# Dilated attention of a two-block model: normalising the outputs instead of the probabilities, in interleaved steps

## The chip, the cores and the metric

The kernel runs on one core of a Trainium2 chip, in one launch. The metric is the device time of that core in microseconds (us), from which the program is judged by the median of several runs. TensorE is called PE here, its weight loads PEld, VectorE DVE, ScalarE ACT, GpSimd POOL and SyncE SP; SP issues most of the transfers (DMAs).

## The reference

The model is two blocks, one after the other, on 1024 tokens of width 1024. The change touches the attention of the second block only: 8 heads of width 64, each a mixture of three causal windows of dilation 1, 4 and 16. The kernel takes the mixture as one softmax per head: the three branches share their scores, and a pair of positions that lies in several branches counts as often, which the kernel puts into a table `bias` of one row set per head (distance times slope, less the logarithm of the count).

```python
for window, dilation in ((128, 1), (512, 4), (2048, 16)):
    s = q·k / 8 + bias                # causal, keys t, t-d, ..., t-window
    m = max(s); p = exp(s - m); denom = sum(p)
    o = (p @ v) / denom;  lse = m + log(denom)
w = softmax(lse over the branches)
attn = sum(w * o over the branches)
```

All products are wanted to nearly full float32 accuracy. The kernel gets it by splitting an operand into a rounded part (type float32r, which PE takes at its fast rate) and the remainder, and adding the products.

## The kernel before

The program works through mixer 1, an MLP, a gate, a feed-forward layer, mixer 2 (where the attention is) and another feed-forward layer. In mixer 2 the projections `qk` and `v`, a state-space part and its gate (`glu`) come ahead of the attention, the output projection (`down`, its first rows at L455) behind it. The method `attention` (L1629) is called once, by `mixer2`.

The order on each engine is found by a scheduler while the program is built: it takes the instructions in the order in which the code issues them as priorities, gives out the buffers of the pools, and writes one fixed queue per engine. At run time each engine takes its queue in order and waits at each instruction for what it needs. So the order of the Python calls, and which pool a tile is in, set the queues.

The tiles come from pools with a fixed number of buffers: `u` (`self.u`, 32 buffers of 128x1024), `t` (`self.tmp`, 5 of 128x512), small ones (`self.sm`), and 8 PSUM banks (`self.bank`). A tile waits until an older one in its pool has been read for the last time.

One pair of heads is one tile `q` and one tile `k` of 128x1024: head `a` = 0 in partitions 0 to 63, `a` = 1 in 64 to 127.

- `heads_in` (L1552) makes, for both heads of a pair at once, the operands of the scores: `qq` holds the rounded queries in the head's own half of the partitions and the remainder in the other half; `kd` holds the rounded keys in both halves, `kl` the remainder of the keys in both. ACT makes the rounded ones (L1560, L1561), POOL the remainders (L1563, L1564), and a DMA brings each key tile's other half (L1562, L1565).
- `head_v` (L1569) makes `vv`, the rounded values of a head and their remainder side by side (ACT L1573, DVE L1574).
- `softmax` (L1577) does half of a head, four blocks of 128 queries, of which block `qb` sees (qb + 1) x 128 keys. Per block: two score matmuls per piece of keys (L1596, L1597), a DVE instruction that adds the bias, writes `P` and keeps the minimum (L1599, the scores are negated), the exponential on ACT with its row sum `den` (L1602), the reciprocal of the sum on DVE (L1603), and the multiplication of the whole row by it on POOL (L1604).
- `values` (L1607) does the output of a half head: for each block of 128 keys (`kt`) it transposes up to four blocks of `P` on PE (L1619), splits the result into `ph` on ACT (L1621) and `pl` on DVE (L1622), and adds two matmuls with `vv` to the bank `po` (L1623, L1624). At the end the two halves of `po` are added into `at` (ACT L1626, DVE L1627).
- `attention` prepares the pair after the current one at each pair's first head, calls `softmax` per half head and holds three `values` jobs back.

The prediction also names L1516, the last multiplication of `glu` (tile `yt`), and L1499 and L1496, which split a tile into `hi` and `lo`.

Of the kernel before, what the change touches and what calls it, by code (L numbers as in the profile page):

```python
# [22 lines left out]
H = 512  # L23
# [89 lines left out]
class Z:  # L113
# [3 lines left out]
    late = "s"  # L117
# [60 lines left out]
class ZS(Z):  # L178
# [4 lines left out]
    late = "u"  # L183
# [64 lines left out]
class Model:  # L248
# [1300 lines left out]
                else:  # L1549
                    self.nc.scalar.activation(o, i, AF.Copy)  # L1550

    def heads_in(self, q, k):  # L1552


        nc = self.nc
        res = []
        for a in range(2):
            me, other = slice(64 * a, 64 * a + 64), slice(64 - 64 * a, 128 - 64 * a)
            qq, kd, kl = self.u("qq", F32R), self.u("kd", F32R), self.u("kl", F32R)
# [17 lines left out]
    def softmax(self, ops, bias, half):  # L1577

        nc = self.nc
        qq, kd, kl = ops  # L1580
        if half:
            ps = [self.u("P") for _ in range(4)]
        else:
            two = [self.u("P", shape=[P, 2, H]) for _ in range(2)]
            ps = [two[c // 2][:, c % 2] for c in range(4)]
        mx, den = self.sm("mx", 8), self.sm("den", 4)
        for c, p in enumerate(ps):
            qb = 4 * half + c
            w = (qb + 1) * P
            o = 896 - qb * P  # L1590
            cuts = [0, w] if w <= H else ([0, 384, w] if w < 896 else [0, H, w])
            init = 3.0e38
            for n, (k0, k1) in enumerate(zip(cuts, cuts[1:])):
                pp = self.bank()[:, : k1 - k0]
                qs = slice(qb * P, (qb + 1) * P)
                nc.tensor.matmul(pp, qq[:, qs], kd[:, k0:k1], start=True, stop=False)  # L1596
                nc.tensor.matmul(pp, qq[:, qs], kl[:, k0:k1], start=False, stop=True)  # L1597
                m = mx[:, c : c + 1] if n == len(cuts) - 2 else mx[:, 4 + c : 5 + c]
                nc.vector.tensor_tensor_reduce(out=p[:, k0:k1], in0=pp, in1=bias[:, o + k0 : o + k1], scale=1.0,  # L1599
                                               scalar=init, op0=ALU.add, op1=ALU.min, accum_out=m)  # L1600
                init = m
            nc.scalar.activation(p[:, :w], p[:, :w], AF.Exp, scale=-1.0, bias=mx[:, c : c + 1], accum_out=den[:, c : c + 1])  # L1602
            nc.vector.reciprocal(den[:, c : c + 1], den[:, c : c + 1])  # L1603
            nc.gpsimd.tensor_scalar(out=p[:, :w], in0=p[:, :w], scalar1=den[:, c : c + 1], scalar2=None, op0=ALU.mult)  # L1604
        return ps

    def values(self, vv, a, ps, half, at):  # L1607


        nc = self.nc  # L1610
        po = self.bank("po")
        me, other = slice(64 * a, 64 * a + 64), slice(64 - 64 * a, 128 - 64 * a)
# [12 lines left out]
        t = self.tmp("vo")  # L1625
        nc.scalar.activation(t[me], po[other], AF.Copy)  # L1626
        nc.vector.tensor_tensor(at[me, half * H : half * H + H], po[me], t[me], op=ALU.add)  # L1627

    def attention(self, qk):  # L1629

        at, late = [], []
        ops = [self.heads_in(*qk[0])]
        for j in range(4):
            at.append(self.u("at"))
            for a in range(2):
                h = 2 * j + a
                bias = self.raw(self.a["bias"][h], name="bias", tag="xr")
                if a == 0 and j < 3:
                    ops.append(self.heads_in(*qk[j + 1]))
                vv = self.head_v(h)  # L1640
# [89 lines left out]
```

## Time and profile before

| | |
|---|---|
| median of 3 runs | 3058.43 us (3047.64 to 3059.11) |
| profiled execution | 3056.01 us, its span 3054.2 us |
| busy in the span | PE 93%, PEld 75%, DVE 59%, ACT 43%, POOL 26% |
| mean granted PE clock | 0.968 of full speed |

The profile shows one execution: each instruction with its engine, start and end, its line in the code and the tiles that it writes and reads (`po<-ph,vv`), the idle time of an engine ahead of an instruction and what ended it. PE is the engine with the most work: 40 slices of the span show it at 0.8 or more nearly all the time, and at 0.7 in two slices side by side near 0.7 of the span, where POOL is at its busiest.

### The profile page before, as it was taken

How to read it: one execution, taken by the hardware profiler on the slowest of the kernel's cores; microseconds unless marked ns; L12 is line 12 of the kernel's file. 1: busy time of each engine (PE TensorE's matmuls, PEld its weight loads, DVE VectorE, ACT ScalarE, POOL GpSimd, SP SyncE). 2: the span in 40 equal slices, each digit the busy share in tenths (PEclk: the TensorE clock that was granted, in tenths of full speed). 3: DMA queues.
4: the chain of work that ended last, by engine and by line, in shares of the span. 5: the costliest groups of instructions: out<-in, count | busy, mean ns of one | idle time of the engine just before them, and what ended most of it. 6: DMA issues, size and time to landing. Idle time of an engine off the chain costs nothing. (4 is left out here: it accounts for less than half of the span.)

```text
span 3054.2 us, 33886 instructions
## 1 busy us (share of the span) xinstructions
PE 2828.5 (93%) x12585; PEld 2303.4 (75%) x12585; DVE 1797.1 (59%) x2561; ACT 1320.1 (43%) x1921; POOL 784.1 (26%) x626
## 2 busy tenths in 40 slices
PE   8998999989979989999989999997789999998997
PEld 7777877767757867778777878886677778777776
DVE  4586655575767366666667561417735756565445
ACT  5446554442335473323324362236655533332343
POOL 3320222200211221111122041349854112111001
PEclk9999999999989999999999999999899899999999
DMA  4114344474466123454466562423113244446645
GB/s 145 57 47 138 131 145 152 156 259 160 166 233 220 56 90 106 153 164 151 164 222 237 207 222 81 155 83 111 42 49 131 87 152 159 159 153 207 225 160 200
DMA packets 198200, 452.93 MB, mean 148 GB/s; under 512 B 20533, under 2 KB 25233, under 8 KB 198033
## 3 DMA queue, kind: packets, MB, share of 16 engines
q1 hardware_dynamic: 193424, 433.97, 41.9%
q10 hardware_dynamic: 4608, 16.78, 1.4%
q8 instruction: 99, 1.62, 0.2%
q14 instruction: 69, 0.56, 0.1%
HBM read 316.51 MB, written 129.99 MB: 146 GB/s over the span
## 5 line engine op out<-in xcount | busy, mean ns | idle before, releaser
L701 PE MATMUL b<-tt,wh 128*128 128x512 f32 x2128 | 686.2, 403 | 74.0 <-ACT tt L687 64.4
L541 PE MATMUL b<-zh,wh 128*128 128x512 f32 x1680 | 646.9, 398 | 35.4 <-ACT wh L481 25.6
L541 PE MATMUL b<-zh,wl 128*128 128x512 f32 x1680 | 625.3, 393 | 4.5 <-ACT wl L511 4.0
L541 PE MATMUL b<-zl,wh 128*128 128x512 f32 x1560 | 615.2, 395 | 8.4 <-DVE zl L211 8.4
L701 PEld LDWEIGHTS b<-tt,wh 128*128 128x128 f32 x2128 | 409.3, 194 | 181.5 <-ACT tt L687 73.8
L701 PE MATMUL b<-tt,wl 128*128 128x512 f32 x1064 | 424.1, 399 | 0.0
L541 PEld LDWEIGHTS b<-zh,wh 128*128 128x128 f32 x1680 | 319.8, 191 | 123.9 <-ACT wh L481 38.8
L541 PEld LDWEIGHTS b<-zh,wl 128*128 128x128 f32 x1680 | 318.2, 190 | 75.5 <-ACT wl L511 6.7
L541 PEld LDWEIGHTS b<-zl,wh 128*128 128x128 f32 x1560 | 296.4, 190 | 73.9 <-DVE zl L211 13.4
L688 DVE TENSOR_TENSOR wl<-sd,wh 128x1024 fp32r<-128x1024 f32 x140 | 167.6, 1197 | 190.3 <-ACT wh L687 190.3
L482 POOL TENSOR_TENSOR wl<-raw,wh 128x1024 fp32r<-128x1024 f32 x51 | 123.3, 2418 | 526.1 <-ACT wh L481 486.6
L701 PEld LDWEIGHTS b<-tt,wl 128*128 128x128 f32 x1064 | 206.7, 194 | 43.6
L481 ACT ACTIVATE wh<-raw 128x1024 fp32r<-128x1024 f32 x120 | 127.2, 1060 | 238.4 <-DMA raw<-in_f_in 95.2
L352 POOL TENSOR_TENSOR wl<-raw,wh 128x1024 fp32r<-128x1024 f32 (+1 forms) x58 | 142.7, 2465 | 322.0 <-ACT wh L351 290.2
L687 ACT ACTIVATE wh<-sd 128x1024 fp32r<-128x1024 f32 x140 | 141.5, 1011 | 154.6 <-DMA sd<-hs 111.9
L383 POOL TENSOR_SCALAR v<-ss 128x1 f32<-128x1 f32 x80 | 47.9, 599 | 472.5 <-ACT junk L376 466.3
L619 POOL TENSOR_TENSOR hw<-h 128x512 f32<-128x512 f32 x38 | 60.2, 1583 | 421.1 <-DVE h L1165 188.1
L687 ACT ACTIVATE tt<-wd 128x1024 fp32r<-128x1024 f32 x92 | 94.6, 1028 | 150.3 <-DVE wd L669 133.1
L505 DVE TENSOR_TENSOR s<-raw 128x512 f32<-128x512 f32 x60 | 82.2, 1370 | 107.5 <-DMA raw<-in_f_in 100.6
L482 DVE TENSOR_TENSOR wl<-raw,wh 128x1024 fp32r<-128x1024 f32 x69 | 88.7, 1286 | 84.2 <-ACT wh L481 43.2
L351 ACT ACTIVATE wh<-raw 128x1024 fp32r<-128x1024 f32 (+1 forms) x58 | 59.5, 1031 | 168.2 <-issue 42.7
L688 DVE TENSOR_TENSOR tt<-wd,tt 128x1024 fp32r<-128x1024 f32 x92 | 110.2, 1198 | 27.6 <-ACT tt L687 26.8
(358 smaller groups left out, 5003.4 us busy)
## 6 DMA issues: line engine op xcount, KB each, us to landing
sd<-hs SPq DMA_DIRECT2D x126, 512.0 KB, 5.5
raw<-in_f_in SPq DMA_DIRECT2D x94, 512.0 KB, 3.7
wd<-in_w_down SPq DMA_DIRECT2D x64, 512.0 KB, 6.3
raw<-in_f_out SPq DMA_DIRECT2D x44, 512.0 KB, 3.6
tw<-raw SPq DMA_DIRECT2D x44, 512.0 KB, 2.9
td<-tw SPq DMA_DIRECT2D x40, 512.0 KB, 6.3
hs<-h SPq DMA_DIRECT2D x38, 512.0 KB, 3.1
hs<-hw SPq DMA_DIRECT2D x38, 512.0 KB, 3.0
```

The source lines that it names most:

```text
L351: nc.scalar.activation(h, r, AF.Copy)
L352: nc.gpsimd.tensor_tensor(l, r, h.bitcast(F32), op=ALU.subtract)
L383: nc.gpsimd.tensor_scalar(out=v, in0=ss, scalar1=1.0 / D, scalar2=EPS, op0=ALU.mult, op1=ALU.add)
L481: nc.scalar.activation(hi.rearrange("p a b -> p (a b)"), x, AF.Copy)
L482: eng.tensor_tensor(lo.rearrange("p a b -> p (a b)"), x, hi.bitcast(F32).rearrange("p a b -> p (a b)"), op=ALU.subtract)
L505: v.tensor_tensor(s1, a21, a22, op=ALU.add)
L541: self.mark = nc.tensor.matmul(bank, w, x, start=start and k == 0 and i == 0, stop=k == 3 and i == 2, skip_group_check=True)
L619: g.tensor_tensor(wt[:, 1], x[:, 1], y[:, 0], op=ALU.subtract)
L687: nc.scalar.activation(hi[:, :n], x[:, :n], AF.Copy)
L688: v.tensor_tensor(lo[:, :n], x[:, :n], hi.bitcast(F32)[:, :n], op=ALU.subtract)
L701: self.mark = nc.tensor.matmul(bank, x[:, c, ts], y[:, c], start=start and k == 0, stop=stop and k == 2, skip_group_check=True)
```

## The change

`heads_in` for a pair becomes `head_in` for one head. It first issues two DMAs that copy the keys of the head to both halves of a float32 tile `k2`; the rest is returned as two functions, one for `qq`, one for `kd` and `kl`, which now cover all 128 partitions and need no DMA behind them. The method `attention` calls these, and `head_v`, one at a time between the steps of the head ahead.

`softmax` and `values` become generators. `attention` advances them by turns: a step of `values` is one block of keys, a step of `softmax` one block of queries. A `values` job now starts two half heads behind its `softmax` (LAG = 2), at most two are pending instead of three.

The probabilities are no longer multiplied. Per half head one POOL instruction takes the reciprocals of `den` (a power with exponent -1, 128x4), a DMA writes them as a row of 512 to DRAM (4 bytes at a time, since it transposes), a second brings that row to all partitions (tile `inv`), and at the end of `values` DVE multiplies the output by it. `ph` and `pl` become the two halves of one tile in the pool of 32.

```diff
+    def head_in(self, q, k, a, res):
+        nc = self.nc
+        me, other = slice(64 * a, 64 * a + 64), slice(64 - 64 * a, 128 - 64 * a)
+        two = self.u("k2")
+        for to in (me, other):
+            nc.sync.dma_start(out=two[to], in_=k[me])
+        def left():
+            qq = self.u("qq", F32R)
             nc.scalar.activation(qq[me], q[me], AF.Copy)
-            nc.scalar.activation(kd[me], k[me], AF.Copy)
-            nc.sync.dma_start(out=kd.bitcast(F32)[other], in_=kd.bitcast(F32)[me])
             nc.gpsimd.tensor_tensor(qq[other], q[me], qq.bitcast(F32)[me], op=ALU.subtract)
-            nc.gpsimd.tensor_tensor(kl[me], k[me], kd.bitcast(F32)[me], op=ALU.subtract)
-            nc.sync.dma_start(out=kl.bitcast(F32)[other], in_=kl.bitcast(F32)[me])
-            res.append((qq, kd, kl))
-        return res
+            res.append(qq)
+        def right():
+            kd, kl = self.u("kd", F32R), self.u("kl", F32R)
+            nc.scalar.activation(kd, two, AF.Copy)
+            nc.gpsimd.tensor_tensor(kl, two, kd.bitcast(F32), op=ALU.subtract)
+            res.extend((kd, kl))
+        return [left, right]
...
@@ softmax
             nc.scalar.activation(p[:, :w], p[:, :w], AF.Exp, scale=-1.0, bias=mx[:, c : c + 1], accum_out=den[:, c : c + 1])
-            nc.vector.reciprocal(den[:, c : c + 1], den[:, c : c + 1])
-            nc.gpsimd.tensor_scalar(out=p[:, :w], in0=p[:, :w], scalar1=den[:, c : c + 1], scalar2=None, op0=ALU.mult)
-        return ps
+            yield
+        nc.gpsimd.tensor_tensor(den, den, self.mone, op=ALU.pow)
+        row = self.pd.tile([4, P], F32, name="den", tag="den", bufs=4)
+        inv = self.tmp("inv")
+        nc.sync.dma_start(out=row.rearrange("c q -> q c"), in_=den)
+        nc.sync.dma_start(out=inv, in_=row.rearrange("c q -> (c q)").partition_broadcast(P))
+        ps.append(inv)
...
@@ values
-            ph, pl = self.tmp("ph", dt=F32R), self.tmp("pl", dt=F32R)
+            both = self.u("ph", F32R, [P, 2, H])
+            ph, pl = both[:, 0], both[:, 1]
...
+            if kt < last:
+                yield
         t = self.tmp("vo")
         nc.scalar.activation(t[me], po[other], AF.Copy)
-        nc.vector.tensor_tensor(at[me, half * H : half * H + H], po[me], t[me], op=ALU.add)
+        nc.vector.tensor_tensor(t[me], po[me], t[me], op=ALU.add)
+        nc.vector.tensor_tensor(at[me, half * H : half * H + H], t[me], ps[4][me], op=ALU.mult)
...
@@ attention
-                for half in range(2):
-                    ps = self.softmax(ops[j][a], bias, half)
-                    late.append((vv, a, ps, half, at[j]))
-                    if len(late) > 3:
-                        self.values(*late.pop(0))
-        while late:
-            self.values(*late.pop(0))
+        for n in range(16 + self.LAG):
...
+            for k in range(nk):
+                if val:
+                    next(val, None)
+                if soft and k * 4 % nk == 0:
+                    next(soft)
+                    if k * 4 // nk in (1, 3) and todo and (half or k * 4 // nk == 1 or len(todo) > 2):
+                        todo.pop(0)()
+            if soft:
+                next(soft, None)
```

What this does to the queues is shown at three places. On POOL, in the first heads, the queue before is a run of multiplications of `P`, with the preparation of a pair (`qq`, `kl`) between two runs:

```order
L1604 TENSOR_SCALAR P<-P,den 128x640
L1604 TENSOR_SCALAR P<-P,den 128x768
L1604 TENSOR_SCALAR P<-P,den 128x896
L1604 TENSOR_SCALAR P<-P,den 128x1024
L1563 TENSOR_TENSOR qq<-qk,qq 64x1024
L1564 TENSOR_TENSOR kl<-qk,kd 64x1024
L1563 TENSOR_TENSOR qq<-qk,qq 64x1024
```

and now it is one preparation step and one power of 128x4 by turns:

```order
L1571 TENSOR_TENSOR kl<-k_15429,kd 128x1024
L1614 TENSOR_TENSOR den<-den,mone 128x4
L1565 TENSOR_TENSOR qq<-qk,qq 64x1024
L1614 TENSOR_TENSOR den<-den,mone 128x4
L1571 TENSOR_TENSOR kl<-k_15639,kd 128x1024
```

All 64 multiplications are gone from it. On PE, at the second half of a head's outputs, the queue before has one block of transposes between the first two output matmuls (`idn` is the identity of a transpose, `kd` and `kl` are score matmuls):

```order
L1623 MATMUL po<-ph,vv 128x512
L1619 MATMUL b<-idn,P 128x128 x21
L1624 MATMUL po<-pl,vv 128x512
L1619 MATMUL b<-idn,P 128x128
L1623 MATMUL po<-ph,vv 128x512
L1624 MATMUL po<-pl,vv 128x512
```

and now (L1639 reads `pl`, which is part of the tile `ph`):

```order
L1638 MATMUL po<-ph,vv 128x512
L1606 MATMUL b<-kd,qq 128x384
L1607 MATMUL b<-kl,qq 128x384
L1606 MATMUL b<-kd,qq 128x256
L1607 MATMUL b<-kl,qq 128x256
L1633 MATMUL b<-idn,P 128x128 x8
L1606 MATMUL b<-kd,qq 128x384
L1607 MATMUL b<-kl,qq 128x384
L1606 MATMUL b<-kd,qq 128x384
L1607 MATMUL b<-kl,qq 128x384
L1639 MATMUL po<-ph,vv 128x512
L1633 MATMUL b<-idn,P 128x128 x8
```

Score matmuls have moved between the transposes. On SP, in the middle of the attention, the queue before holds bias tables and key copies only:

```order
L1562 DMA kd<-kd 64x1024 x2
L307 DMA bias<-in_bias 128x1024
L1565 DMA kl<-kl 64x1024 x2
L307 DMA bias<-in_bias 128x1024
```

and now, per head, two transfers of the reciprocals to DRAM (`den`, 128x4 in single elements), each with the broadcast that needs it (`inv`):

```order
L1617 DMA den<-den 128x4x1
L1618 DMA inv<-den 128x512
L1560 DMA k_15639<-qk 64x1024 x2
L307 DMA bias<-in_bias 128x1024
L1617 DMA den<-den 128x4x1
L1618 DMA inv<-den 128x512
```

The key copies and bias tables of later heads stand behind an `inv`, which waits for its `den` to land.

## Rows read from the trace of the kernel before

**Rows 1.** The page's 40 equal slices of the span: busy tenths of PE.
```profile
PE   8998999989979989999989999997789999998997
```

**Rows 2.** Timeline, last two jobs of `values`: start, us, instruction, idle before it.
```profile
2239.98 0.33 PE L1624 MATMUL po<-pl,vv 128*128 128x128 f32 x1
...
2253.02 0.69 DVE L1627 TENSOR_TENSOR at<-po,vo 64x512 f32<-64x512 f32 x1 [1.04 <-ACT vo L1626]
```

**Rows 3.** Stretches: us, then busy PE, PEld, DVE, ACT, POOL; clock, DMA share, GB/s.
```profile
2118.00:2140.00 22.00, 18.79 (x113) 16.25 (x112) 19.57 (x64) 15.99 (x38) 21.59 (x12) 1.00 0.19 49
2157.00:2180.00 23.00, 19.45 (x114) 16.52 (x112) 19.65 (x61) 16.62 (x38) 22.59 (x13) 1.00 0.19 46
2140.00:2157.00 17.00, 10.24 (x55) 8.84 (x53) 10.57 (x31) 13.73 (x28) 17.00 (x10) 0.80 0.23 62
2203.00:2230.00 27.00, 21.29 (x127) 17.96 (x127) 23.21 (x75) 20.48 (x48) 19.15 (x11) 1.00 0.12 40
2079.84:2252.40 172.56, 127.47 (x674) 107.08 (x672) 124.06 (x377) 122.18 (x263) 144.79 (x79) 0.89 0.19 58
```

**Rows 4.** Groups by line, POOL, 2080 to 2253: count, busy us, mean ns, idle before.
```profile
L1604 POOL TENSOR_SCALAR P<-P,den 128x640 f32<-128x640 f32 (+5 forms) x64 | 109.5, 1734 | 11.9 <-DVE den L1603 11.0 <-PE b L1597 0.7
L1563 POOL TENSOR_TENSOR qq<-qk,qq 64x1024 fp32r<-64x1024 f32 x4 | 9.9, 2471 | 0.3
```

**Rows 5.** Waits, 2080 to 2253, PE and ACT: us in total, times, longest.
```profile
PE po L1623 <- ACT ph L1621: 34.0, 17, 5.0
PE b L1619 <- POOL P L1604: 5.8, 3, 3.7
ACT ph L1621 <- PE po L1624: 18.7, 31, 2.1
```

**Rows 6.** Timeline, POOL and PE, 2095 to 2120.
```profile
2095.37 24.53 POOL L1604 TENSOR_SCALAR P<-P,den 128x512 f32<-128x512 f32 x13
...
2109.05 0.33 PE L1619 MATMUL b<-idn,P 128*128 128x128 f32 x1 [3.71 <-POOL P L1604]
```

**Rows 7.** Timeline, ACT and PE, 2146 to 2152.
```profile
2146.74 1.04 ACT L1560 ACTIVATE qq<-qk 64x1024 fp32r<-64x1024 f32 x1
...
2149.71 1.04 ACT L1561 ACTIVATE kd<-qk 64x1024 fp32r<-64x1024 f32 x1
...
2151.43 0.79 PE L1623 MATMUL po<-ph,vv 128*128 128x512 f32 x1 [4.98 <-ACT ph L1621]
```

**Rows 8.** Two lines of the code (POOL, DVE): count, duration ns min/median/max, first and last start.
```profile
L384 POOL TENSOR_TENSOR r<-v,mh x80: 547/548/1627, 6.5 to 3045.9; 128x1 f32<-128x1 f32 x80
...
L1574 DVE TENSOR_TENSOR vv<-v,vv x8: 677/1045/2328, 2062.7 to 2209.0; 128x512 fp32r<-128x512 f32 x8
```

**Rows 9.** Timeline, DVE, 2088 to 2094.
```profile
2088.20 0.15 DVE L1603 RECIPROCAL den<-den 128x1 f32<-128x1 f32 x1
2088.28 0.53 DVE L1599 CUSTOM_DVE_ANT_0 P<-b,bias 128x384 f32<-128x384 f32 x1
...
2093.20 0.74 DVE L1599 CUSTOM_DVE_ANT_0 P<-b,bias,mx 128x512 f32<-128x512 f32 x1
```

**Rows 10.** Groups by line, DVE, 2080 to 2253.
```profile
L1627 DVE TENSOR_TENSOR at<-po,vo 64x512 f32<-64x512 f32 x15 | 10.3, 686 | 9.1 <-ACT vo L1626 9.0
L1516 DVE TENSOR_TENSOR yt<-gs,yt 128x512 f32<-128x512 f32 x3 | 6.0, 1986 | 1.2 <-ACT gs L1515 1.2
```

**Rows 11.** DMA issues of the whole program: KB each, median us to landing.
```profile
raw<-in_pT SPq DMA_DIRECT2D x2, 512.0 KB, 10.2
s5l<-kz SPq DMA_DIRECT2D x64, 32.0 KB, 2.2
dsk<-in_s5d SPq DMA_DIRECT2D x1, 2.0 KB, 9.1
g<-in_rows SPq DMA_DIRECT2D x3, 512.0 KB, 3.9
```

**Rows 12.** Timeline, SP, one issue.
```profile
2093.98 0.33 SPq L307 DMA_DIRECT2D bias<-in_bias  x1
```

More of the change, by code (lines that the diff above doesn't have):

```diff
@@ L1550, in v_proj @@
                     self.nc.scalar.activation(o, i, AF.Copy)
-    def heads_in(self, q, k):
+    def head_in(self, q, k, a, res):
         nc = self.nc
[L1556 to L1559, printed above, removed]
+        me, other = slice(64 * a, 64 * a + 64), slice(64 - 64 * a, 128 - 64 * a)
[4 more added lines that the diff above has]
+            qq = self.u("qq", F32R)
             nc.scalar.activation(qq[me], q[me], AF.Copy)
-            nc.scalar.activation(kd[me], k[me], AF.Copy)
-            nc.sync.dma_start(out=kd.bitcast(F32)[other], in_=kd.bitcast(F32)[me])
             nc.gpsimd.tensor_tensor(qq[other], q[me], qq.bitcast(F32)[me], op=ALU.subtract)
-            nc.gpsimd.tensor_tensor(kl[me], k[me], kd.bitcast(F32)[me], op=ALU.subtract)
-            nc.sync.dma_start(out=kl.bitcast(F32)[other], in_=kl.bitcast(F32)[me])
-            res.append((qq, kd, kl))
-        return res
+            res.append(qq)
[5 more added lines that the diff above has]
+        return [left, right]
     def head_v(self, h):
@@ L1575, in head_v, with softmax @@
         return vv
-    def softmax(self, ops, bias, half):
+    def softmax(self, ops, bias, half, ps):
         nc = self.nc
@@ L1581, in softmax @@
         if half:
-            ps = [self.u("P") for _ in range(4)]
+            ps.extend(self.u("P") for _ in range(4))
         else:
             two = [self.u("P", shape=[P, 2, H]) for _ in range(2)]
-            ps = [two[c // 2][:, c % 2] for c in range(4)]
+            ps.extend(two[c // 2][:, c % 2] for c in range(4))
+        four = list(ps)
         mx, den = self.sm("mx", 8), self.sm("den", 4)
-        for c, p in enumerate(ps):
+        for c, p in enumerate(four):
             qb = 4 * half + c
@@ L1624, in values @@
             nc.tensor.matmul(po[:, sl], vv[:, kt, :], pl[:, sl], start=False, stop=kt == last)
+            if kt < last:
+                yield
         t = self.tmp("vo")
         nc.scalar.activation(t[me], po[other], AF.Copy)
-        nc.vector.tensor_tensor(at[me, half * H : half * H + H], po[me], t[me], op=ALU.add)
+        nc.vector.tensor_tensor(t[me], po[me], t[me], op=ALU.add)
+        nc.vector.tensor_tensor(at[me, half * H : half * H + H], t[me], ps[4][me], op=ALU.mult)
+    LAG = 2
@@ L1629, in attention @@
     def attention(self, qk):
[L1631 to L1640, printed above, removed]
-                for half in range(2):
-                    ps = self.softmax(ops[j][a], bias, half)
-                    late.append((vv, a, ps, half, at[j]))
-                    if len(late) > 3:
-                        self.values(*late.pop(0))
@@ L1646, in attention, with prepare @@
-        while late:
-            self.values(*late.pop(0))
+        nc = self.nc
+        self.mone = self.sm("mone", 4)
+        nc.vector.memset(self.mone, -1.0)
+        at, late, heads = [], [], {}
+        def prepare(h):
+            ops, vv = [], []
+            bias = self.raw(self.a["bias"][h], name="bias", tag="xr")
+            heads[h] = ops, bias, vv
+            return [*self.head_in(*qk[h // 2], h % 2, ops), lambda: vv.append(self.head_v(h))]
+        for f in prepare(0):
+            f()
@@ new lines, in attention @@
+        for n in range(16 + self.LAG):
+            h, half = divmod(n, 2)
+            soft = None
+            if h < 8:
+                if half == 0:
+                    if h % 2 == 0:
+                        at.append(self.u("at"))
+                    todo = prepare(h + 1) if h < 7 else []
+                ops, bias, vv = heads[h]
+                ps = []
+                soft = self.softmax(ops, bias, half, ps)
+                late.append((vv[0], h % 2, ps, half, at[h // 2]))
+            val, nk = None, 4
+            if n >= self.LAG:
+                job = late.pop(0)
+                val, nk = self.values(*job), 4 + 4 * job[3]
+            for k in range(nk):
[7 more added lines that the diff above has]
+                next(soft, None)
```

## The prediction

> **What bounds the kernel now.** I read the table of slices first, to find where the tensor engine (PE) is not full. Nearly everywhere it is; the one place with two slices side by side at 0.7 is the 28th and 29th of the 40 [rows 1], some 76 us each, and there lies the attention, from 2079.84 us (the first score matmul) to 2253.71 us (the last output sum, 2253.02 + 0.69 [rows 2]): 173.9 us of the 3054.2 us span. The view by stretches [rows 3] says what the engines did in it: PE 127.47 us, DVE 124.06, ACT 122.18 and POOL 144.79 busy. In three stretches, together 72 us, DVE gets 62.43 / 72 = 0.867 of the time, though in two of them POOL has hardly a gap; the PE clock there is 1.00, its upper level of 2.4 GHz. Between them lie stretches such as 2140 to 2157, where POOL is busy for all 17.00 us, PE for 10.24 and DVE for 10.57, and the clock is 0.80, a mean over both levels (1.2 and 2.4 GHz).
>
> Next the groups by line say what POOL does: the 64 multiplications of the probabilities (L1604) take 109.5 us [rows 4]. The waits say who suffers [rows 5]: PE stands 34.0 us for `ph` on ACT, and 5.8 us for `P` on POOL; ACT stands 18.7 us before `ph`, for the last matmul that reads an older `ph` or `pl`, since these two, `vo` and other things share five buffers. The timeline shows how the waits join [rows 6]: POOL runs 13 multiplications without a break from 2095.37 for 24.53 us, and PE, which takes its instructions in order, stands 3.71 us at a transpose of `P`; the score matmuls behind it stand too. A second knot is the preparation of two heads in one block [rows 7]: ACT makes `qq`, `kd`, `qq`, `kd` from 2146.74 to 2150.75, the `ph` that PE needs comes behind them, and PE stands 4.98 us.
>
> So POOL sets the pace of the softmax, and the outputs trail: three jobs of `values` are left when the last probabilities are done, and the last two alone take from the end of the one before (2239.98 + 0.33) to 2253.71, 13.4 us [rows 2].
>
> **The change, part by part.**
> (1) Removed from POOL: 109.5 us. Added there: 16 powers of 128x4; the nearest row, a power of 128x1, takes 547 ns [rows 8], so some 9 us, spread over the stage. With these and the `qq` and `kl` of seven heads, some 35 us, POOL is busy for about a third of the stage and stops being a bound. `qq` and `kl` cost what they did (2471 ns [rows 4]; `kl` doubles its partitions, not its columns).
> (2) DVE loses 64 reciprocals. Each takes 0.15 us, but the next instruction starts 0.08 us behind its start [rows 9], so they give back 64 x 0.08 = 5.1 us. It gains 16 multiplications of 64x512. The nearest row is the 64x512 sum of L1627 at 686 ns [rows 10]: 16 x 0.69 = 11.0 us. Both operands now lie in SBUF, though, and `vv`, the nearest row with that, runs from 677 ns to 2328 ns, median 1045 [rows 8]; I take 0.69 since POOL is mostly idle by then, and keep 1.04 for the range.
> The Trainium skill (GPSIMD Engine Reference, Specifications) says that POOL shares its SBUF interfaces with VectorE and contends with instructions that read two SBUF tensors; the spread of `vv` agrees. By that rule the emptier POOL makes both cheaper than before, so it supports the lower figure.
> (3) ACT keeps its work. Six `qq` and `kd` copies of three heads that used to be made ahead of the stage now fall into it: at most 6 x 1.04 = 6.3 us [rows 7]. They come one at a time between other instructions, so the second knot goes.
> (4) `ph` and `pl` in the pool of 32: the 18.7 us of ACT waits [rows 5] can go. If that pool were full at this point they would come back.
> (5) PE has the same instructions. Its order is finer: 21 transposes stood in one block behind a `ph` matmul, now 8 and 8 stand between score matmuls, and their `P` is two halves of a head old when they run.
> (6) SP gets, per half head, a transfer of the 128x4 reciprocals into a row in DRAM, in pieces of 4 bytes, and one of that row to all partitions (256 KB), which must wait for the first. The copies of the keys stay 16 of 256 KB. Nothing in the trace moves 4-byte pieces. Bounds from the nearest rows: 2.2 us (64 pieces of 512 B) and 9.1 us (16 pieces of 128 B, the same 2 KB), 10.2 us for the slowest landing of any [rows 11]. I take 4 us, nearer the lower, since the stage leaves the transfers idle for most of the time (DMA share 0.19 over the stage [rows 3]). The second is like the row broadcast of 512 KB, 3.9 us at most [rows 11]. The row is wanted at the end of `values`, nearly two half heads later (some 17 us): 0.55 + 4 + 3.9 is hidden, and 0.55 + 9.1 + 3.9 = 13.6 still is. SP holds the bias and the keys of later heads behind it; these have the same slack.
>
> **The sum.** With POOL out of the way DVE and ACT bound the stage, both nearly equal. DVE's work: 124.06 - 6.0 (the three `yt` of the preceding stage [rows 10], which lie at the start) - 5.1 + 11.0 = 124.0 us, 15.5 per head. ACT has at most (122.18 + 6.3) / 8 = 16.1, some of which belongs to no head. How densely they can be packed I read from the best stretches, 0.867, which also hold PE waits and `ph` waits: 15.5 / 0.867 = 17.9 us per head. The stage is then the start, until head 0's score reductions are done, some 12 us (they end at 2093.9 [rows 9], with about 2 us for another head between them), seven heads of 17.9 = 125.3, and the last two jobs of `values`, 13.4 + 0.69 for the new multiplication = 14.1: 151.4 us against 173.9. That is 22.5 us less. The profiled execution took 3056.01 us, 2.4 below the median of 3058.43: 3056.0 - 22.5 = 3033.5, say **3034 us**.
>
> **Rivals.**
> - *The three engines pack better.* The clock stays up, ACT no longer waits for buffers. At 0.95: 16.3 per head, stage 140, 3022 us. For it: PE's stalls lay at POOL. Against: DVE and ACT need each other twice per tile. Chance 0.16.
> - *The waits move rather than go.* PE, ACT and DVE are all near 0.7 of the stage now; their in-order queues may hold each other as POOL did, or `ph` finds the big pool full. From 2118 to 2157, knot included, DVE got (19.57 + 10.57) / 39 = 0.773: 20.05 per head, stage 166.5, 3049 us; with the multiplication at 1.04, 16 x 0.35 / 0.773 = 7 more, 3056. For it: no stretch of the trace shows above 0.89. Against: both knots that the trace shows are taken apart. Chance 0.25.
> - *SP becomes the bound, and the kernel is slower.* The broadcast waits for the 4-byte transfer, and the next half head's transfer is queued behind it. One turn of SP is the landing time X and two issues of 0.33 us [rows 12] and half of three more for keys and bias, X + 1.2. If that is longer than a half head, DVE stands at the multiplication, with the score reductions behind it. Sixteen turns from about 2090, then 3.9 and 0.7: the stage ends at 2113.8 + 16 X, the old end at X = 8.7. At 10.2 us it ends at 2277, 23.3 later: 3079 us. For it: the 2 KB row at 9.1 us. Against: that one ran at the start of the program beside big loads. Chance 0.07. The Trainium skill (DMA: Bandwidth & Descriptors, Specifications) has a rule on this side: pieces under 512 B are written by reading and modifying, so these would be the slowest kind. No row here shows 4 bytes; the page gives no time for it.
> - *It does what it says and still gains nothing*, since ACT or DVE takes all that POOL gave: packing as over the whole stage, 0.719, gives 21.6 per head, 3057 us. This is the far end of the second rival and shares its chance.
>
> **How the numbers follow.** Forecast 0.52, better packing 0.16, moved waits 0.25, SP 0.07. About half a percent, 15 us, is what a measurement of this kernel can tell from no change; so faster means below 3043.1. All of the first two lie there and a little of the third: 0.70. The rest of the third is the same: 0.23. SP at X near 10 and mishaps beside it: 0.07 slower. The range takes in better packing with a shorter tail, 3018, and the moved waits with the dearer multiplication, 3056.
>
> **What would show it.** Right: no L1604; POOL below 0.4 in the stage; PE waits for `ph` well under 34 us; DVE at about 0.85 of the stage between its ends; the clock at 1.00 in most 10 us slices; a stage of 145 to 158 us; the rest of the program as long as before. Wrong: waits of DVE for `inv` (SP), waits of ACT's `ph` for a matmul as large as before (pool), a stage above 165 us, or a landing of the 4-byte transfer above 8 us.

## The result and the profile after

| | before | after |
|---|---|---|
| median of 4 runs each | 3058.77 us (3047.64 to 3059.50) | 3098.47 us (3094.35 to 3101.41) |
| ratio, 95% interval | | 1.0137 (1.0112 to 1.0163) |
| profiled execution, its span | 3056.01, 3054.2 us | 3098.23, 3096.3 us |
| attention: first score matmul to last output | 173.7 us | 212.7 us |
| from there to the end | 800.5 us | 807.3 us |

The change makes the kernel 40 us slower; the forecast was 3034 us, and 3098 lies outside its range of 3018 to 3056. (The first score matmul of the kernel before starts at 2080.06; at the prediction's 2079.84 its weight load starts, so the stage there was 173.7 us and not 173.9.) Of the 42.1 us between the two spans the attention has 39.0 and the part behind it 6.8; the attention begins 3.7 us earlier.

The view by stretches of the kernel after, for the whole stage and three stretches of it (columns as in [rows 3]):

```profile
2076.27:2289.00 212.73, 139.40 (x673) 113.26 (x672) 128.48 (x329) 123.95 (x268) 59.53 (x34) 0.83 0.38 65
...
2100.00:2120.00 20.00, 16.63 (x86) 13.33 (x85) 15.26 (x40) 17.00 (x37) 6.76 (x4) 0.91 0.23 23
...
2140.00:2160.00 20.00, 12.37 (x51) 9.99 (x49) 10.45 (x26) 7.61 (x16) 2.39 (x1) 0.67 0.35 66
...
2275.00:2290.00 15.00, 2.00 (x12) 1.55 (x10) 3.62 (x7) 5.03 (x8) 7.49 (x3) 0.65 0.34 62
```

POOL has 59.53 us of work instead of 144.79 [rows 3], as it was meant to. Yet no other engine took over: PE is at 0.66 of the stage, DVE at 0.60, ACT at 0.58. From 2140 to 2160 all of them are half idle. An engine that bounds a stage is busy in it; here none is, so the bound is a wait. PE's 139.40 us for the same matmuls that took 127.47 go with a lower granted clock, 0.83 in the mean instead of 0.89: 0.91 from 2100 to 2120, where PE is busy for 16.63 of 20 us, and 0.67 from 2140 to 2160, where it stands for 7.41 us on end and is busy for 12.37. The share of the transfer engines has doubled, to 0.38.

The waits of the kernel after, 2076 to 2290 (us in total, times, longest), of all engines and of SP's queue:

```profile
POOL kl L1571 <- ACT kd L1570: 70.1, 6, 16.1
DVE at L1645 <- DMA inv<-den: 54.6, 11, 9.5
...
ACT P L1612 <- DVE mx L1609: 48.3, 13, 13.1
PE po L1639 <- DVE ph L1637: 42.8, 21, 8.0
...
PE po L1638 <- ACT ph L1636: 16.5, 19, 3.4
...
SPq L1618 <- DMA den<-den: 165.0, 16, 13.3
```

The 34.0 us in which PE stood for `ph` on ACT [rows 5] have become 16.5, and no wait of ACT's `ph` for an older matmul is left of the 18.7. In their place DVE stands 54.6 us at the last multiplication for `inv`, and what stands behind it in DVE's queue is waited for by ACT (48.3, the score minimum) and PE (42.8, the remainder `pl`, part of the tile `ph`). The last line is the source: SP stands 165.0 us, at each of the 16 broadcasts, for the reciprocals ahead of it to land. Source lines L1617 and L1618 give the landing times:

```profile
L1617 SPq DMA_DIRECT2D den<-den x16: 372/402/1300, 2084.2 to 2272.8; - x16
...
DMA to landing us min/median/max: 8.4/10.8/14.0
...
L1618 SPq DMA_DIRECT2D inv<-den x16: 319/319/326, 2092.6 to 2283.5; - x16
...
DMA to landing us min/median/max: 3.8/5.0/8.2
```

So X, the landing time of the 4-byte transfer, is 10.8 us. How a turn of SP becomes a stall shows in the timelines of SP and then of all engines at one place:

```profile
2133.00 0.39 SPq L1617 DMA_DIRECT2D den<-den  x1
2144.18 0.32 SPq L1618 DMA_DIRECT2D inv<-den  x1
2144.59 1.11 SPq L1560 DMA_DIRECT2D k<-qk  x2
2145.79 0.56 SPq L307 DMA_DIRECT2D bias<-in_bias  x1
2146.44 1.19 SPq L1617 DMA_DIRECT2D den<-den  x1
2157.54 0.32 SPq L1618 DMA_DIRECT2D inv<-den  x1
```

```profile
2149.31 0.68 DVE L1645 TENSOR_TENSOR at<-vo,inv 64x512 f32<-64x512 f32 x1 [7.11 <-DMA inv<-den]
...
2150.65 0.80 PE L1639 MATMUL po<-ph,vv 128*128 128x512 f32 x1 [7.41 <-DVE ph L1637]
2151.74 0.83 ACT L1612 ACTIVATE P<-P,mx 128x640 f32<-128x640 f32 x1 [13.13 <-DVE mx L1609]
...
2154.65 2.39 POOL L1571 TENSOR_TENSOR kl<-k,kd 128x1024 fp32r<-128x1024 f32 x1 [16.14 <-ACT kd L1570]
```

SP issues `den` at 2133.00, stands 10.8 us, issues `inv` at 2144.18, then the keys, the table and the next `den`, and stands again. The row lands 5 us after its issue; DVE, in order, waits 7.11 us, and PE, ACT and POOL each stand behind it. The first broadcast goes out at 2092.59 and the last at 2283.50: 15 turns of 190.9 / 15 = 12.7 us.

### The profile page after: what moved, and what is told of

Read it like the earlier page. It is cut to its first block, busy times and chain, and to the rows that moved or that the text cites. A ratio compares the mean times of both kernels' runs of the same rounds, so it can differ in the third digit from the quotient of the medians.

```text
span 3096.3 us, 33763 instructions
## 1 busy us (share of the span) xinstructions
PE 2842.8 (92%) x12585; PEld 2311.1 (75%) x12585; DVE 1787.9 (58%) x2514; ACT 1317.9 (43%) x1921; POOL 689.2 (22%) x578
```

## The experiments

All build on one of the two kernels. Theory A is the prediction's third rival, that SP's turn is the bound. The table gives each kernel's median, its ratio to the kernel before on the same chip (interval in brackets; a single execution has none), the stage from the first score matmul to the last output, and the median X. Stage and X are those of one profiled execution, which can lie some us from the median: e2's took 3035.8 us, e5's 3048.1.

| run | us | ratio | stage | X |
|---|---|---|---|---|
| e1 keys and tables first | 3073.2 | 1.0055 (1.0040 to 1.0071) | 192.2 | 10.4 |
| e2 no transfers | 3041.9 | 0.9949 (0.9934 to 0.9964) | 150.5 | |
| e3 new order, POOL as before | 3050.2 | 0.9971 (0.9960 to 0.9983) | 166.1 | |
| e4 old order, row | 3092.5 | 1.0120 (1.0101 to 1.0138) | 210.2 | 10.8 |
| e5 16-byte pieces | 3040.8 | 0.9939 (0.9925 to 0.9952) | 153.7 | 1.6 |
| e6 128 of 4 bytes | 3153.9 | one execution | 264.2 | 14.3 |
| e7 two in flight | 3061.1 | 1.0011 (1.0001 to 1.0021) | 176.1 | 8.6 |
| e8 scaled identity | 3058.0 | 1.0004 (0.9991 to 1.0018) | 166.0 | |
| e9 128 of 4 bytes, same row | 3068.7 | one execution | 183.9 | 9.0 |
| e10 `ph` in the small pool | 3052.4 | 0.9988 (0.9976 to 1.0000) | 170.8 | 1.4 |
| e11 old order, row, 16 bytes | 3053.4 | 0.9988 (0.9977 to 0.9999) | 172.9 | 1.4 |
| e12 one job back, 16 bytes | 3074.2 | 1.0053 (1.0040 to 1.0066) | 194.3 | 1.4 |
| e13 4 bytes, 512 apart | 3034.1 | one execution | 149.5 | 1.8 |
| e14 4 bytes side by side | 3037.6 | one execution | 151.5 | 7.1 |
| e15 traffic alone | 3037.9 | 0.9937 (0.9918 to 0.9957) | 150.4 | 9.5 |

### e1: the broadcast later in SP's queue

```diff
-        nc.sync.dma_start(out=inv, in_=row...partition_broadcast(P))
         ps.append(inv)
+        ps.append(lambda: nc.sync.dma_start(out=inv, in_=row...partition_broadcast(P)))
...
+            if late and len(late[0][2]) > 5:
+                late[0][2].pop()()
             if soft:
                 next(soft, None)
```

> Only the place of the row broadcasts in SP's queue changes: each is issued one half head later, so that SP finds its reciprocals landed. Theory A (SP's turns: every half head SP stands for the landing of the reciprocals, 165.0 us in all, and the next half head's reciprocals, the keys and the bias stand behind it): SP's wait for `den` falls below 30 us, DVE's wait for `inv` from 54.6 to below 15 us, the stage from 213 us to 150 to 165, the kernel to 3034 to 3050 us. Theory B (the finer order itself makes PE, ACT and DVE wait for one another): the stage stays above 195 us, the kernel above 3080. Theory C (the latency of one row, 10.8 + 5.0 us, is on the path however SP's queue is ordered): `inv` comes even later, DVE's wait stays above 50 us, the kernel at 3095 or more.

It lies between the theories: 25 us less than the change, still slower than before, with 130.8 us of SP's waits for `den` and 43.7 of DVE's for `inv`, which fit neither A nor C. SP's timeline shows why:

```profile
2109.70 0.32 SPq L1619 DMA_DIRECT2D inv<-den  x1
2110.11 0.39 SPq L1617 DMA_DIRECT2D den<-den  x1
2110.59 1.11 SPq L1560 DMA_DIRECT2D k<-qk  x2
2112.99 0.34 SPq L307 DMA_DIRECT2D bias<-in_bias  x1
2120.56 0.33 SPq L1619 DMA_DIRECT2D inv<-den  x1
```

Keys and table now go out ahead of the wait, but only one transfer of reciprocals is ever under way: each `inv` still stands between two `den`. The turn is X and two issues, (2266.82 - 2096.77) / 15 = 11.3 us, still more than the half head of 9 us that the forecast had. My expectation overlooked that X alone is longer than a half head: a later place in the queue that is still ahead of the next `den` could not hide it.

### e2: no transfers

```diff
-        row = self.pd.tile([4, P], F32, name="den", tag="den", bufs=4)
-        inv = self.tmp("inv")
-        nc.sync.dma_start(out=row.rearrange("c q -> q c"), in_=den)
-        nc.sync.dma_start(out=inv, in_=row...partition_broadcast(P))
-        ps.append(inv)
+        ps.append(self.one)
@@ attention
+        self.one = self.u("one", shape=[P, 2, H])[:, 0]
+        nc.gpsimd.memset(self.one, 0.0625)
```

> The two transfers per half head are left out; the multiplication at the end of `values` stays and reads a constant, so the outputs are not normalised. Theory A: as the run with the later rows, 3034 to 3050 us, at most 8 us faster than that one if 8192 small pieces also slow the key copies. Theory B: above 3080 us. Theory C: 3034 to 3050 us too, but then far below the run with the later rows.

The time is the one of theories A and C, and against B: the finer order does not slow the stage. That it lies 31 us below e1, where A allowed 8, was C's forecast and not A's; e4 has to part the two. Its stage is 150.5 us where the prediction's sum had 151.4:

```profile
2079.29:2229.83 150.54, 124.69 (x673) 106.41 (x671) 131.66 (x329) 124.22 (x268) 58.31 (x34) 0.89 0.23 63
...
2091.00:2213.00 122.00, 106.35 (x572) 91.90 (x571) 104.80 (x278) 100.42 (x224) 43.12 (x26) 0.89 0.20 52
```

Between its ends DVE has 104.80 / 122 = 0.859, against 0.867 in the sum. The two transfers cost 3098.5 - 3041.9 = 57 us.

### e3 and e4: each half of the change alone

e3 keeps the change's order and normalises on POOL; e4 keeps the order of before and normalises by the row.

```diff
@@ e3, softmax of the kernel after
+            nc.vector.reciprocal(den[:, c : c + 1], den[:, c : c + 1])
+            nc.gpsimd.tensor_scalar(out=p[:, :w], in0=p[:, :w], scalar1=den[:, c : c + 1], scalar2=None, op0=ALU.mult)
             yield
-        nc.gpsimd.tensor_tensor(den, den, self.mone, op=ALU.pow)
...
-        nc.sync.dma_start(out=row.rearrange("c q -> q c"), in_=den)
-        nc.sync.dma_start(out=inv, in_=row...partition_broadcast(P))
...
@@ e4, softmax of the kernel before
-            nc.vector.reciprocal(den[:, c : c + 1], den[:, c : c + 1])
-            nc.gpsimd.tensor_scalar(out=p[:, :w], in0=p[:, :w], scalar1=den[:, c : c + 1], scalar2=None, op0=ALU.mult)
+        nc.gpsimd.tensor_tensor(den, den, self.mone, op=ALU.pow)
...
+        nc.sync.dma_start(out=row.rearrange("c q -> q c"), in_=den)
+        nc.sync.dma_start(out=inv, in_=row...partition_broadcast(P))
...
```

In both the last lines of `values` change to fit: e3 ends with the sum, e4 multiplies it by `inv`, which lies in the pool of 32 there.

> The changed order, key copies and pools, but the probabilities normalised on POOL as in the kernel before (reciprocal on DVE, multiplication on POOL, no power, no transfers, no last multiplication). Theory A: no turn of SP, POOL has its 110 us again beside 35 us of `qq` and `kl`; the knots of the old order are gone, so the stage is between 155 and 176 us, the kernel between 3038 and 3060. Theory B: slower than the kernel before by over 20 us, 3080 or more.

> The kernel before, its blocks and its order, with three jobs held back and `ph` and `pl` in the pool of 5, but the probabilities left as they are and the outputs multiplied by the row of reciprocals, through the same two transfers. Theory A: the same turns of SP, 16 of about 12.5 us and the key copies and bias behind them: the stage is 195 to 225 us, the kernel 3080 to 3105. Theory B: the old order with POOL freed is faster than before, 3035 to 3050. Theory C: three jobs held back give more slack, 3045 to 3065.

Both came as theory A said. e3 has the 64 multiplications again and is still 0.29% faster than the kernel before: the order, with the key copies and pools that came with it, is worth 7.5 us of stage. e4 shows the same turns in the old order, and nearly the same loss; theories B and C fall. Its waits, of SP's queue and then of DVE:

```profile
SPq L1607 <- DMA den<-den: 157.8, 16, 11.8
...
DVE P L1599 <- DMA bias<-in_bias: 24.3, 4, 11.5
DVE at L1632 <- DMA inv<-den: 20.4, 5, 6.5
```

Three jobs held back shorten DVE's wait for the row (54.6 us in the change) but not the loss: DVE now stands as long for the bias tables, which wait behind the row in SP's queue. It is a rate that is missed, not a delay.

### e5: pieces of 16 bytes

```diff
-        row = self.pd.tile([4, P], F32, ...)
+        row = self.pd.tile([P, 4], F32, ...)
-        nc.sync.dma_start(out=row.rearrange("c q -> q c"), in_=den)
-        nc.sync.dma_start(out=inv, in_=row.rearrange("c q -> (c q)").partition_broadcast(P))
+        nc.sync.dma_start(out=row, in_=den)
+        nc.sync.dma_start(out=inv, in_=row.rearrange("q c -> (q c)").partition_broadcast(P))
@@ values: at, t seen as (c q), inv as (q c)
-        nc.vector.tensor_tensor(at[...], t[me], ps[4][me], op=ALU.mult)
+        nc.vector.tensor_tensor(c4(at[...]), c4(t[me]), ps[4][me].rearrange("p (q c) -> p c q", c=4), op=ALU.mult)
```

> The reciprocals go to DRAM as they lie, 128 pieces of 16 bytes instead of 512 of 4, and the last multiplication reads the row in steps of four; queue order as in the change. Theory P (the landing time X grows with the number of pieces, since the transfer engines work them off one by one, and key copies wait behind them): X falls from 10.8 to 4 to 5 us, the key copies land in under 5 us, SP's turn is shorter than a half head, the stage 148 to 158 us (the run without transfers had 149), the kernel 3040 to 3052. Theory L (any transfer of pieces this small takes some 10 us, however many): X stays above 9 us, the kernel above 3085.

The same 2 KB now land in 1.6 us (L1617), and DVE has no wait for `inv` left:

```profile
DMA to landing us min/median/max: 1.4/1.6/3.1
```

This is the fastest full version of the study: 18 us below the kernel before on the same chip, 58 below the change. The strided multiplication costs 1.09 us instead of 0.69 in the median. Theory P had the kernel's time right and X too high (it said 4 to 5 us), a first sign that the number of pieces is not the measure. (Its 149 us for the run without transfers stop 1.3 us before the end of the last multiplication; the stage there is 150.5.)

### e7: two transfers under way

```diff
@@ softmax
-        nc.sync.dma_start(out=row.rearrange("c q -> q c"), in_=den)
+        self.den = nc.sync.dma_start(out=row.rearrange("c q -> q c"), in_=den)
...
+        def bring(mine=self.den):
+            d = nc.sync.dma_start(out=inv, in_=row...partition_broadcast(P))
+            if self.den is not mine:
+                self.after(d, self.den)
+        ps.append(bring)
@@ attention
             if soft:
                 next(soft, None)
+            if late and len(late[0][2]) > 5:
+                late[0][2].pop()()
```

`self.after` only orders the two in SP's queue.

> 512 pieces of 4 bytes as in the change, but from the second half head on SP issues the next reciprocals before it waits for the older ones, so that two transfers are under way at once. Theory P: the engines are the limit, not SP's waiting; two at once slow each other, X rises to 13 us or more, and the turn of two issues of `inv` stays near 10 us: stage above 175 us, kernel 3060 to 3080. Theory L: X stays near 10.8 us, the turn falls to the half head's 9 us, the stage to 150 to 160 and the kernel to 3042 to 3055.

Neither fits. The landing of L1617, SP's wait and DVE's:

```profile
DMA to landing us min/median/max: 7.8/8.6/10.8
...
SPq L1620 <- DMA den<-den: 41.7, 9, 9.8
...
DVE at L1649 <- DMA inv<-den: 26.3, 9, 4.5
```

The transfers overlap in pairs: the second of a pair is issued 4 to 6 us after the first (once 0.5), and 8.6 us is the median landing of all. So an overlap of some 3 to 4 us does not slow them visibly (against P), and SP's wait for `den` fell from 165.0 to 41.7 us; but the stage is 176.1, not 150 to 160: the broadcasts land in 7.3 us, among the small pieces, and DVE still waits 26.3 us for `inv`. Two under way take back 36.6 of the 62.2 us by which the change's stage is longer than e2's.

### e6, e9, e13, e14: what makes X long

All send only the first column of the reciprocals, 128 pieces of 4 bytes. In e6 the row is that column four times, in e9 it is read as in the change, in e13 and e14 a constant row that waits for nothing is read.

```diff
@@ e9
+        nc.sync.dma_start(out=row[0:1].rearrange("c q -> q c"), in_=den[:, 0:1])
@@ e13: row is a tile of [128, 128] in DRAM
+        nc.sync.dma_start(out=row[:, 0:1], in_=den[:, 0:1])
@@ e14: row is [1, 128]
+        nc.sync.dma_start(out=row.rearrange("c q -> q c"), in_=den[:, 0:1])
```

> Only the first of the four columns of reciprocals is sent, 128 pieces of 4 bytes, and the row is that column four times (so the outputs are multiplied by the wrong reciprocals for three blocks of four). Theory P: X as in the run with 128 pieces of 16 bytes, 4 to 5 us, and the kernel within 8 us of that run. Theory L: X above 9 us, above 3085. If the size of a piece matters and not the number, X lies above 9 here and below 6 there.

> 128 pieces of 4 bytes again, but the row is read exactly as in the change (its other three quarters hold a constant, written ahead of the stage, so three blocks of four are multiplied by that). Theory P (the number of pieces): X is 2 to 4 us, a quarter of the 8.6 us that the change's transfer takes with no broadcast ahead of it, and the kernel 3040 to 3060. Theory S (pieces of 4 bytes are slow, 128 as well as 512): X is 7 us or more, the kernel above 3080.

> 128 pieces of 4 bytes, each written 512 bytes from the next; the row that the outputs are multiplied by is a constant that waits for nothing, so this run prices the landing X alone. Theory S1 (a piece of 4 bytes is slow by its size): X stays at 7 to 9 us. Theory S2 (many pieces written into the same 512 bytes hinder each other: 128 of them took 9.0 us, 32 of 16 bytes 1.4 to 1.6): X falls to 1.4 to 2.5 us.

> The control for the pieces 512 bytes apart: 128 pieces of 4 bytes side by side, 512 bytes in all, again with a constant row that waits for nothing. Both theories: X 7 to 9 us, as in the run with a quarter of the pieces. If it is below 3 us here, what made X long there was the broadcast ahead of it and not the pieces.

e6 went off by its own edit: the broadcast, now in four parts per partition, took 9.6 us instead of 5.0, and the reciprocals behind it 14.3; it tells little of X. e9 is the clean form: a quarter of the pieces, and X (L1618 there) is 9.0 us, as theory S said, though the kernel, at 3068.7, is faster than S's 3080.

```profile
DMA to landing us min/median/max: 8.3/9.0/12.7
```

Theory P falls. The landings of L1617 in e13 and e14 then part the two readings of S:

```profile
DMA to landing us min/median/max: 1.4/1.8/2.9
```

```profile
DMA to landing us min/median/max: 6.0/7.1/10.3
```

The same 128 pieces of 4 bytes land in 1.8 us when each is written 512 bytes from the next (first line, e13) and in 7.1 us side by side (e14). S2 holds: neither the number of pieces nor their size alone makes the price, but that many are written close together. Why that costs, no run shows.

### e15: the traffic without the wait

As e14, but with the change's whole transfer of 512 pieces, `out=row.rearrange("c q -> q c"), in_=den`.

> The change's transfer of 512 pieces of 4 bytes, still issued for each half head, but the row is a constant, so SP never waits for it. If SP's wait for the landing is what costs the time, the kernel is within 8 us of the run without transfers (3042), 3038 to 3052, with X at 8 to 9 us. If the traffic itself slows the key copies, tables and broadcasts so that others wait: above 3060.

X, the landing of L1617, is 9.5 us and nothing waits for it: 3037.9 us, as without transfers.

```profile
DMA to landing us min/median/max: 7.9/9.5/12.7
```

So the 57 us are lost by the waits for the landing, SP's and DVE's behind it, and the traffic itself costs nothing that can be told.

### e8: normalising while turning

```diff
+            nc.vector.reciprocal(den[:, c : c + 1], den[:, c : c + 1])
+            nc.gpsimd.tensor_scalar(out=dgs[:, c], in0=self.idn, scalar1=den[:, c : c + 1], scalar2=None, op0=ALU.mult)
...
-                nc.tensor.transpose(pp[...], ps[c][...], self.idn)
+                nc.tensor.matmul(pp[...], ps[c][...], ps[4][:, c], start=True, stop=True)
```

> No transfers and no last multiplication: the identity by which PE turns the blocks of `P` is multiplied by the reciprocals (64 times 128x128 on POOL, 64 reciprocals on DVE), and a plain matmul with it turns and normalises at once. POOL has 64 x 0.5 to 0.6 = 35 us more than in the run without transfers, still under half of the stage. If a plain float32 matmul of 128x128 takes what the turning took (0.32 us), the stage is 145 to 158 us and the kernel 3038 to 3050; if it takes twice that, PE has 49 us more and bounds the stage: 180 to 200 us, 3070 to 3090.

Between the two cases: 3058.0 us, no gain. The group of the turning matmuls on PE (count, busy, mean ns, idle before):

```profile
L1632 PE MATMUL b<-dg,P 128*128 128x128 f32 x576 | 81.1, 284 | 2.4 <-POOL dg L1616 2.0 <-DVE mx L1610 0.2
```

The 288 turnings are now recorded as 576 matmuls and take 81.1 us, overlaps counted once, where the 288 transposes of the kernel before took 49.0: 32 us more on PE. The stage is 166.0.

### e10, e11, e12: the other parts, with the cheap transfer

e10 puts `ph` and `pl` back into the pool of 5 (and `inv` into that of 32). e11 is e4 with the transfer of e5. e12 is e5 with `LAG = 1`.

> The kernel with 16-byte pieces, with `ph` and `pl` back in the pool of 5 (and `inv` in the pool of 32). If the pool cost what the trace of the kernel before showed, ACT waits 10 to 19 us for matmuls that read an older `ph` or `pl`, and the kernel is 6 to 15 us slower than with 16-byte pieces alone, 3047 to 3056. If those waits came from the old order, the two agree within 4 us.

> The kernel before with its order and pools, outputs multiplied by the row, the reciprocals sent as 128 pieces of 16 bytes. If POOL was what bound the old order: the stage is 150 to 163 us and the kernel 3040 to 3052, 40 to 50 below the same kernel with 4-byte pieces. If the blocks of the old order (21 transposes at once, two heads prepared at once) cost as much by themselves: 3053 to 3062.

> The kernel with 16-byte pieces, and a job of `values` one half head behind its softmax instead of two. One job less is left at the end: 5 to 8 us less, 3033 to 3038. The other way: the transposes meet exponentials that have only just been made and the row comes 6 to 7 us after its power, inside the same half head; then PE waits for `P` by over 15 us and the kernel is at 3041 to 3055.

e10 lies 4.3 us below the kernel before on its chip, e5 18.1 on its own: as much is lost as the waits had suggested, but not by the wait that I named. ACT's `ph` waits only 4.5 us for a matmul. The waits of ACT's `ph` in e10 and then in e5:

```profile
ACT ph L1635 <- PE b L1633: 24.1, 19, 2.7
...
ACT ph L1635 <- PE po L1638: 4.5, 6, 2.4
```

```profile
ACT ph L1636 <- PE b L1633: 7.7, 8, 1.9
```

ACT waits for transposes instead. The blocks of 21 are not back: but for two at the end (10 and 20), no run of transposes in e10's PE queue is longer than 8, while eight of the kernel before have 19 to 21. Since the pool also decides the finer order in which the scheduler puts the instructions, whether the want of buffers or that order costs the time stays open. e11 is a miss of its first case: POOL is freed, the transfer is cheap, and the stage is 172.9 us, 0.8 below that of the kernel before. Its 3053.4 us lie at the edge of the second case, but e10, without the blocks, has nearly the same stage, 170.8; so the blocks are not shown to be the reason. e12 is as slow as feared, and more: PE waits for the exponential of the half head just done (e12, then e5).

```profile
PE b L1633 <- ACT P L1612: 37.7, 22, 5.3
...
PE b L1633 <- ACT P L1612: 1.3, 4, 0.5
```

Of the two distances tried, two half heads is the better one.

## Why the prediction was wrong

**The failed step is part (6), the landing of the 4-byte transfer.** The prediction took X = 4 us from bounds of 2.2 and 10.2 us; it is 10.8, above both. The rows that gave the bounds [rows 11] are loads out of DRAM, two of them in pieces of 512 and 128 bytes; none writes many small pieces side by side into DRAM, and e13 and e14 show that just this is what costs. With 4 us taken as hidden, the sum has no term for it; the runs put it at 62.2 us of stage (212.7 against e2's 150.5). The third rival had the mechanism, the place and the price: "the stage ends at 2113.8 + 16 X". With 10.8 that is 2286.6; the last output ended at 2289.0. At 16 x 0.6 us more than its 3079 it gives 3089; the 9 us that are missing are these 2.4 and the 6.8 us in the part behind the attention. That the end of the stage comes out so close is partly luck: a turn took 12.7 us and not X + 1.2 = 12.0, and the first transfer went out at 2084.2 and not at about 2090. Its chance of 0.07 was too small by the prediction's own numbers: the break-even was 8.7 us, and a row of the same 2 KB had taken 9.1 [rows 11]. I set that row aside because it ran beside big loads, without a row that showed the load to be the reason.

**The slack argument was of the wrong kind.** Part (6) held that 0.55 + 9.1 + 3.9 = 13.6 us is hidden, since the row is wanted some 17 us later. That is true of one row, and useless: e4 holds three jobs back and loses nearly as much. SP makes one turn per half head and waits in it, so what has to fit is the turn, X + 1.2 by the rival and 12.7 us as measured, into the half head's 9 us (8.7 in e2, from its first to its last multiplication, 15 half heads).

The Trainium skill (DMA: Bandwidth & Descriptors, Specifications) has pieces under 512 B read and written back; the prediction gave that rule as a reason why these would be the slowest kind. The size of a piece alone does not give the time here: pieces of 16 bytes land in 1.6 us and pieces of 4 bytes, set apart, in 1.8. Whether many such pieces in one stretch hinder each other by being read and written back, no run shows.

**Right: what the stage would be without that wait.** "151.4 us against 173.9": 150.5 without transfers, 153.7 with 16-byte pieces, 150.4 with the traffic alone; DVE's share 0.859 against the 0.867 taken. POOL fell to 0.28 of the longer stage, 0.39 in e2 (58.31 of 150.54; forecast: below 0.4). The kernel gains 18 us with e5 where 22.5 was forecast, its stage is 2.3 us longer than the sum, and the part behind the stage took 805.7 us in its profiled execution instead of 800.5. One sign failed even without the wait: the clock, which was to be 1.00 in most 10 us slices, is so in four of e2's fifteen from 2080 to 2230, and 0.89 in the mean, as before; PE is busy for 0.83 of that stage, as near a bound as DVE with 0.87 and ACT with 0.83, the two that the sum named.

**Half right: that POOL sets the pace.** POOL freed in the old order and pools gives 0.8 us of stage (e11), the new order and pools with POOL loaded 7.5 (e3), both together 20.0 (e5), and POOL freed in the new order with `ph` and `pl` in the pool of 5 2.8 (e10). Each is one execution, so 0.8 and 2.8 cannot be told from each other or from nothing. So POOL's work bounds the stage side by side with something that the new order alone (e10) does not take away and the new order with the large pool does; removing either one lets the other decide. The knots in PE's and ACT's queues [rows 6, 7] are not that something by themselves, since e10 has neither them nor a loaded POOL. The old order with the large pool was not tried. The prediction read the first from busy time alone (144.79 of 172.56) and would have promised most of the 22 us for e11 as well.

**The smaller terms.** The powers take 1.01 us each, not 0.55, and only SP waits for them. The multiplication at the end of `values` takes 0.69 us in the median, as part (2) took it; the source line L1645 of the kernel after (duration ns min/median/max):

```profile
L1645 DVE TENSOR_TENSOR at<-vo,inv x16: 683/689/1264, 2097.6 to 2288.3; 64x512 f32<-64x512 f32 x16
```

Beside a busy POOL it is dearer. In e2 POOL runs four instructions from 2224.18 for 10.20 us, and the last two multiplications take 2.68 and 1.99 us there:

```profile
2224.18 10.20 POOL L1499 TENSOR_TENSOR lo<-at,hi 128x1024 fp32r<-128x1024 f32 x4 [6.06 <-PE po L1634]
...
2224.40 2.68 DVE L1641 TENSOR_TENSOR at<-vo,one 64x512 f32<-64x512 f32 x1
...
2227.84 1.99 DVE L1641 TENSOR_TENSOR at<-vo,one 64x512 f32<-64x512 f32 x1
```

The Trainium skill (GPSIMD Engine Reference, Specifications) says that POOL contends with VectorE instructions that read two SBUF tensors; these rows agree. The sign "the rest of the program as long as before" was missed in the profiled execution: 807.3 us behind the stage against 800.5. The other kernels lie between 797.0 (e4) and 807.7 (e3), e15 with the changed order at 800.4. The four executions of the kernel before differ by 11.9 us among themselves, so these few us are not shown to come from the change. Two slips of the prediction's own numbers change nothing: its last rival's 21.6 us per head give 3059 us and not 3057, and DVE is above 0.89 in single 10 us slices of the kernel before (busy for all of 2160 to 2170).

## What to carry to other kernels

Where a queue waits in it for a transfer, compare the length of its whole turn with the period of the loop: slack of several periods hides a delay, not a rate. Before sending a column as single elements side by side, look whether the tile can go as it lies and the reader take the step instead; here that turned a loss of 40 us into a gain of 18. Where two limits stand side by side, as POOL's work and the order with its pools did here, the gain of removing one is read from a run, not from its busy time.

## What the runs showed of the hardware

How long the small transfer takes depends on where its pieces are written, in medians of 16 landings:

| pieces | written | X, us |
|---|---|---|
| 512 of 4 bytes | side by side, 2 KB | 8.6 to 10.8 |
| 128 of 4 bytes | side by side, 512 bytes | 7.1 (e14); 9.0 (e9) and 14.3 (e6) with a broadcast ahead |
| 128 of 4 bytes | 512 bytes apart | 1.8 |
| 128 of 16 bytes | side by side, 2 KB | 1.4 to 1.6 |

So 128 pieces in one stretch of 512 bytes take 7 us, 32 in each of four stretches 1.5. Over how many bytes pieces hinder each other, and by what, the runs don't show. A plain float32 matmul of 128x128 (e8) shows in the trace as two of 284 ns in the mean, a transpose of the kernel before as one of 317; these overlap, and 288 of each keep PE busy for 81.1 and 49.0 us.
